# Sharing the last split row of a relu-and-sum kernel between ScalarE and VectorE, and cutting it in other places

## The chip, the cores and the metric

One core of a Trainium2 chip runs the whole program. Times are device microseconds (us) of that core. The span in the profile, from the first to the last recorded work of one execution, is shorter than the time by more than a microsecond. Engines are named as the profile names them: ACT is ScalarE, DVE is VectorE, SP is SyncE, which issues all transfers here.

## The reference

```
x: float32 [32, 512, 1024]            # 64 MiB
out = sum(max(x, 0), axis=-1)         # float32 [32, 512]
```

The 16,384 rows of 1,024 columns are laid over 128 partitions, so each partition has 128 rows. The last 16 of them, row 0 to row 15 below, are the last block, which the change is about.

## The kernel before

Seven loads of 16 rows (8 MiB) keep the transfer queue full. ScalarE clamps, VectorE sums, or either engine does both for one row with an accumulator output. The last block arrives in smaller and smaller loads, so that little work is left when the last bytes land: 8 rows, 4 rows, rows 12 and 13 with the first 360 columns of row 14, then row 15, then the rest of row 14 in pieces of 260 and 404 columns. Row 14 is the split row. VectorE sums its parts one after another; the closing instruction reads the last piece and, in the two columns behind it, the partial sums of the other parts (never negative, so the clamp leaves them as they are).

```
TAIL = [8, 4]
PIECES = [360, 260, 404]
...
    def dve_row(ap, accum_out, loaded):      # clamp and sum in one instruction
        i = nc.vector.tensor_scalar(out=ap, in0=ap, scalar1=0.0, scalar2=None,
                                    op0=MAX, op1=ADD, accum_out=accum_out)
        if loaded is not None:
            i.wait_op(loaded, 16, "sem-ge")
        i.then_inc(sems.dve, 1)
...
    first = PIECES[0]
    loaded = load(... rows 12, 13 and the first 360 columns of row 14 ...)
    act_row(buf[:, c, :], m, loaded)                              # row 12
    dve_row(buf[:, c + 1, :], res[:, m + 1 : m + 2], loaded)      # row 13
    last_loaded = load(buf[:, c + 3, :], rows(m + 3, 1)[:, 0, :]) # row 15
    arrived = []
    for part, w in zip(parts, PIECES[1:]):                        # 260, 404
        arrived.append(load(part[:, :w], rows(m + 2, 1)[:, 0, col : col + w]))
        col += w
    sums_done = n_act, n_dve
    act_row(buf[:, c + 3, :], m + 3, last_loaded)                 # row 15
    store(0, ROWS, *freed[0])
    store(ROWS, NT - ROWS - 2, *sums_done)
    last, w = parts[-1], PIECES[-1]
    dve_row(buf[:, c + 2, :first], last[:, w : w + 1], None)      # 360 columns
    for i in range(1, extra):
        dve_row(parts[i - 1][:, :], last[:, w + i : w + i + 1], arrived[i - 1])
    nc.vector.wait_ge(sems.dve, n_dve)        # own partial sums are written
    nc.vector.tensor_scalar(...last...).wait_op(arrived[-1], 16, "sem-ge")
    store(NT - 2, 2, n_act, n_dve)            # the last two results
```

## Time and profile before

| | before |
|---|---|
| time, median of 3 runs (range) | 161.35 us (161.24 to 161.53) |
| profiled execution: time, span | 160.99, 159.6 us |
| load queue's share of the transfer engines' time | 98.1% |
| VectorE, ScalarE busy | 74%, 65% |
| rows 12 and 13 land; row 13 starts | 155.34; 155.36 us |
| end of VectorE, end of ScalarE | 158.17, 157.81 us |

A load **lands** when its semaphore tells the waiting engine that the bytes are there. I call **the tail** the time from the start of row 13 on VectorE to the end of VectorE's last accumulator read: 158.17 - 155.36 = 2.81 us. The lines themselves, read from the end backwards, are in the prediction.

### The profile page before, as it was taken

The numbers are of one execution on the slowest core, as the hardware profiler recorded it, in microseconds if no ns is written. First come the engines' busy times: TensorE is split into PE (matmuls) and PEld (weight loads), VectorE is DVE, ScalarE is ACT, GpSimd is POOL, SyncE is SP. The second block draws the span as 40 slices with busy tenths as digits, with TensorE's granted clock in tenths as the row PEclk, the third lists the DMA queues.
The fourth block names the chain that finished last, engine by engine and source line by source line (L and its number), as shares of the span: only waits on it lengthen the run. The fifth ranks groups of instructions, "written<-read, shape, count | busy, mean of one in ns | idle before, by whom it ended". The sixth has DMA issues, their size and how long they took to land.

```text
span 159.6 us, 129 instructions
## 1 busy us (share of the span) xinstructions
DVE 117.5 (74%) x41; ACT 104.2 (65%) x50; POOL 0.2 (0%) x4
## 2 busy tenths in 40 slices
DVE  0000000009999499994999999999999999999986
ACT  3000059990799708996099941999339992499985
POOL 0000000000000000000000000000000000000000
DMA  7996996996996998979969969969969969798994
GB/s 263 525 525 263 525 526 263 525 525 263 526 493 296 525 411 378 525 328 460 526 279 509 525 263 526 525 263 525 525 263 525 509 279 525 337 452 386 412 405 127
DMA packets 2304, 67.18 MB, mean 421 GB/s; under 512 B 640, under 2 KB 896, under 8 KB 1024
## 3 DMA queue, kind: packets, MB, share of 16 engines
q1 hardware_dynamic: 2304, 67.18, 98.1%
HBM read 67.11 MB, written 0.07 MB: 421 GB/s over the span
## 4 chain that ended last, share of the span: by engine, by line
DMA 43%; DVE 34%; ACT 17%; another core or an unknown queue 3%; SPq 0%; issue 0%; DVEq 0%
DMA io<-in_x_dram 43%; DVE res L123 32%; ACT io L115 17%; DVE io L140 1%; SPq L97 0%; DVE piece L219 0%; DVE piece L140 0%; DVEq L218 0%
## 5 line engine op out<-in xcount | busy, mean ns | idle before, releaser
L123 DVE TENSOR_REDUCE res<-io 128x8 f32<-128x8192 f32 (+2 forms) x9 | 101.1, 11286 | 39.9 <-ACT io L115 39.9
L115 ACT ACTIVATE io<-io 128x8192 f32<-128x8192 f32 (+2 forms) x9 | 81.7, 9111 | 46.9 <-DMA io<-in_x_dram 46.9
L130 ACT ACTIVATE io<-io 128x1024 f32<-128x1024 f32 x20 | 20.9, 1045 | 5.9 <-DMA io<-in_x_dram 5.7
L140 DVE TENSOR_SCALAR_CACHE_REDUCE io<-io 128x1024 f32<-128x1024 f32 (+1 forms) x14 | 15.5, 1165 | 0.7 <-DMA io<-in_x_dram 0.6
L130 ACT ACTIVATION_READ_ACCUMULATOR io<-io 128x1 f32 x20 | 3.8, 188 | 0.0
L115 ACT ACT_TABLE_LOAD x1 | 1.3, 1283 | 0.8 <-PEq L260 0.8
L140 DVE DVE_READ_ACCUMULATOR io<-io 128x1 f32 x14 | 1.2, 82 | 0.0
L219 DVE TENSOR_SCALAR_CACHE_REDUCE piece<-piece 128x406 f32<-128x406 f32 x1 | 0.6, 576 | 0.1
L140 DVE TENSOR_SCALAR_CACHE_REDUCE piece<-piece 128x260 f32<-128x260 f32 x1 | 0.4, 424 | 0.0
L260 POOL MEMSET const-bfloat16-1.0<- 128x1 bf16 x1 | 0.1, 102 | 0.0
L260 POOL MEMSET const-uint8-127<- 128x1 uint8 x1 | 0.1, 102 | 0.0
L260 POOL MEMSET const-float32-0.0<- 128x1 f32 x1 | 0.1, 99 | 0.2 <-issue 0.2
L260 POOL MEMSET const-float32-1.0<- 128x1 f32 x1 | 0.1, 99 | 0.0
L140 DVE DVE_READ_ACCUMULATOR piece<-piece 128x1 f32 x1 | 0.1, 83 | 0.0
L219 DVE DVE_READ_ACCUMULATOR piece<-piece 128x1 f32 x1 | 0.1, 82 | 0.0
## 6 DMA issues: line engine op xcount, KB each, us to landing
io<-in_x_dram SPq DMA_DIRECT2D x1, 4096.0 KB, 21.6
io<-in_x_dram SPq DMA_DIRECT2D x1, 2048.0 KB, 26.1
io<-in_x_dram SPq DMA_DIRECT2D x1, 1204.0 KB, 28.6
io<-in_x_dram SPq DMA_DIRECT2D x1, 512.0 KB, 29.4
piece<-in_x_dram SPq DMA_DIRECT2D x1, 202.0 KB, 29.3
piece<-in_x_dram SPq DMA_DIRECT2D x1, 130.0 KB, 29.3
io<-in_x_dram SPq DMA_DIRECT2D x7, 26.9
out_dram<-res SPq DMA_DIRECT2D x1, 55.0 KB, 1.6
```

Source lines behind the costliest of these rows:

```text
L115: i = nc.scalar.activation(out=ap, in_=ap, func=RELU)
L123: nc.vector.tensor_reduce(out=res[:, m : m + n], in_=ap, axis=mybir.AxisListType.X, op=ADD).wait_op(sems.act, n_act, "sem-ge").then_inc(se ...
L130: i = nc.scalar.activation(out=ap, in_=ap, func=RELU, accum_out=res[:, m : m + 1])
L140: i = nc.vector.tensor_scalar(out=ap, in0=ap, scalar1=0.0, scalar2=None, op0=MAX, op1=ADD, accum_out=accum_out,)
L219: nc.vector.tensor_scalar(out=last[:, :], in0=last[:, :], scalar1=0.0, scalar2=None, op0=MAX, op1=ADD, accum_out=res[:, NT - 2 : NT - 1],) ...
L260: nc = _bacc.Bacc("TRN2", target_bir_lowering=False, num_devices=1)
```

## The change

The intent: ScalarE has a hole between row 12 and row 15. Let it take 180 columns of row 14 there, so that VectorE has less to do, and let the closing instruction be shorter (228 columns instead of 406). The load with rows 12 and 13 now brings 390 columns of row 14 (180 for ScalarE, 210 for VectorE), the last 190 columns come with row 15 in one load (they lie side by side in memory), and the middle comes last, as 220 and 224 columns.

```
-PIECES = [360, 260, 404]
+ACT_PIECE, DVE_PIECE, END_PIECE = 180, 210, 190
+PIECES = [220, 224]
...
+    loaded = load(flat[:, at : at + b], src[:, :b])            # rows 12, 13, 390 columns
+    act_row(buf[:, c, :], res[:, m : m + 1], loaded)
+    sums_act = n_act
+    act_row(flat[:, at + split : at + a], others[0], None)     # 180 columns, ScalarE
+    piece_act = n_act
+    dve_row(buf[:, c + 1, :], res[:, m + 1 : m + 2], loaded)
+    sums_dve = n_dve
+    dve_row(flat[:, at + a : at + b], others[1], None)         # 210 columns
+    loaded = load(flat[:, at + end : at + 4 * D], src[:, end:])# 190 columns and row 15
+    act_row(buf[:, c + 3, :], res[:, m + 3 : m + 4], loaded)
+    nc.vector.wait_ge(sems.act, piece_act)                     # ScalarE's partial sum
+    dve_row(flat[:, at + end : at + 3 * D], others[2], loaded) # 190 columns
...
-    dve_row(buf[:, c + 2, :first], last[:, w : w + 1], None)
-    for i in range(1, extra):
-        dve_row(parts[i - 1][:, :], last[:, w + i : w + i + 1], arrived[i - 1])
+    for i in range(len(PIECES) - 1):
+        dve_row(parts[i][:, :], others[3 + i], arrived[i])     # 220 columns
     nc.vector.wait_ge(sems.dve, n_dve)
... (closing instruction: 224 columns and four partial sums)
```

## The prediction

> **What bounds the kernel now.** I read first the page's busy shares and DMA table. VectorE is busy for 74% of the span, ScalarE for 65%, and the load queue for nearly all of it:
>
> ```profile
> q1 hardware_dynamic: 2304, 67.18, 98.1%
> ```
>
> The columns are packets, megabytes and the share of the 16 transfer engines' time. 67.11 MB must be read whatever is done at the end. The change moves not one byte of it. So only the tail, between the landing of the last bytes and the end of the last store, can shrink. I read that next, in the timeline from 155 us on (start, duration, engine, line, operation, output<-input, shapes):
>
> ```profile
> 155.36 1.06 ACT L130 ACTIVATE io<-io 128x1024 f32<-128x1024 f32 x1 [0.45 <-DMA io<-in_x_dram]
> 155.36 1.22 DVE L140 TENSOR_SCALAR_CACHE_REDUCE io<-io 128x1024 f32<-128x1024 f32 x1 [0.57 <-DMA io<-in_x_dram]
> ...
> 156.50 0.52 DVE L140 TENSOR_SCALAR_CACHE_REDUCE io<-io 128x360 f32<-128x360 f32 x1
> ...
> 156.65 1.06 ACT L130 ACTIVATE io<-io 128x1024 f32<-128x1024 f32 x1
> ...
> 157.02 0.42 DVE L140 TENSOR_SCALAR_CACHE_REDUCE piece<-piece 128x260 f32<-128x260 f32 x1
> 157.37 0.08 DVE L140 DVE_READ_ACCUMULATOR piece<-piece 128x1 f32 x1
> 157.58 0.58 DVE L219 TENSOR_SCALAR_CACHE_REDUCE piece<-piece 128x406 f32<-128x406 f32 x1
> 157.62 0.19 ACT L130 ACTIVATION_READ_ACCUMULATOR io<-io 128x1 f32 x1
> 158.09 0.08 DVE L219 DVE_READ_ACCUMULATOR piece<-piece 128x1 f32 x1
> ```
>
> The reader is to see that after the landing at 155.34 VectorE goes straight through row 13 and the three parts of row 14 (360, 260, then 404 columns with the two partial sums), and ends at 158.17. ScalarE has row 12, a hole of 0.15 us, row 15, and ends at 157.81, 0.36 us before VectorE. The last store starts after VectorE's end and lands 1.4 us later, at 159.6. Only the last VectorE end matters, as long as ScalarE stays before it.
>
> Third, when each piece landed. The issue of each piece, from two short windows of the timeline, and the list of issues (KB, us from issue to landing):
>
> ```profile
> 127.73 0.45 SPq L97 DMA_DIRECT2D piece<-in_x_dram  x1
> ```
> ```profile
> 128.22 0.50 SPq L97 DMA_DIRECT2D piece<-in_x_dram  x1
> ```
> ```profile
> piece<-in_x_dram SPq DMA_DIRECT2D x1, 202.0 KB, 29.3
> piece<-in_x_dram SPq DMA_DIRECT2D x1, 130.0 KB, 29.3
> ```
>
> So 260 columns land at 127.73 + 29.3 = 157.03, and the last 404 at 128.22 + 29.3 = 157.52. The same sum gives 155.34 for the load with rows 12 and 13 (issued 126.77, the chain's 28.57 us) and 156.65 for row 15 (issued 127.25, 29.4 us), and both are where the waiting instructions start. Last, the end of the chain that ended last:
>
> ```profile
> 157.47 0.03 issue
> 157.49 0.02 DVEq L218
> 157.51 0.07 issue
> 157.58 0.58 DVE piece L219 x2
> ```
>
> VectorE's own queue was ready for the last instruction at 157.51, the data at 157.52 within the rounding. **Two limits meet there:** the kernel before is balanced between transfer and VectorE, and taking from one alone is not enough.
>
> **What the Trainium skill says.** "ScalarE: Activation LUTs", section What ACT_TABLE_LOAD costs, gives 186 ns + 0.833 ns per column for an ACTIVATE without pointer operands, and an overlap of about 93 ns back to back. The trace agrees: 1042 ns for 1024 columns against 1039 ns; with the accumulator read of 187 ns starting 0.95 us in, rows repeat every 1.04 us. "VectorE: DVE Perf Modes", section The TRN2 errata, says that each instruction on SBUF pays a fixed extra latency, so many small pieces pay it many times. The trace has it: 424, 523, 576 and 1214 ns for 260, 360, 406 and 1024 columns is about 155 ns + 1.035 ns per column. Section The DRAIN says that a semaphore between two instructions of VectorE costs nothing extra; here I go by the trace, which differs: from the end of the 260 columns' accumulator read (157.45) to the start of the last instruction is 0.13 us, though part of that may be the landing at 157.52. "DMA: Bandwidth & Descriptors", Anatomy of one DMA, says a transfer's semaphore fires only after its last byte is confirmed; the trace shows load traffic falling to 10 GB/s by 157.0 to 157.2 us, with the landing at 157.52.
>
> **The change part by part.** I need VectorE's start-to-start step, not its duration. 1024 columns step by 1.14 us, and the accumulator read, which marks where the next may start, comes 0.45 us after the 360 columns and 0.35 us after the 260. That is 0.07 us + 1.045 ns per column.
>
> *Landings.* From 155.34 to 157.52, the remaining 512 + 130 + 202 KB landed, 864,256 bytes in 2.18 us, 396 GB/s. With this rate:
> - the first load now carries 390 columns instead of 360 of row 14, 15,360 bytes more: 155.34 + 0.04 = 155.38;
> - the second, 190 + 1024 columns, is 621,568 bytes, 1.57 us: 156.95 (row 15 landed at 156.65 before, so 0.30 us later);
> - 220 columns, 112,640 bytes, 0.28 us: 157.23;
> - 224 columns, 0.29 us: 157.52, as before, for the bytes are the same.
>
> *ScalarE.* Row 12 starts at 155.40; the 180 columns start 1.04 us later, at 156.44, and take 0.186 + 0.150 = 0.34 us; their accumulator read starts 0.09 us before that ends and takes 0.19, so the partial sum is there at 156.88. It was idle then, so this is **free**: it ends before 156.95. Row 15 then runs from 156.97 and by the same shape as before (1.16 us from start to the end of its read) ends at 158.13.
>
> *VectorE.* Row 13 at 155.40, the 210 columns at 156.54, done at 156.54 + 0.07 + 0.22 = 156.83. Now comes the new wait for ScalarE's 180 columns, passed at about 156.90; with the 0.02 us wait instruction and 0.07 us to the next start that the old wait shows, the 190 columns start at about 156.99, close to the 156.97 at which the data would allow it. They step by 0.27: 157.26. The 220 columns are there since 157.23, start at 157.26 and step by 0.30, and their accumulator read ends at 157.26 + 0.30 + 0.08 = 157.64. The old 0.13 us for the wait on the own partial sums gives 157.77. The last instruction has 224 + 4 = 228 columns, 0.07 + 0.24 = 0.31 us, and its read 0.08: **158.16, against 158.17 before.**
>
> *Sum.* ScalarE takes 180 x 1.045 ns = 0.19 us off VectorE. One more piece gives 0.07 us back. The rest goes to waits: before, row 14's first two parts ran in the time until 157.5 and no transfer held them by more than 0.07 us; now the 190 columns start about 0.15 us after VectorE could take them, since their load arrives with row 15's bytes. The last instruction starts 0.19 us later than before and is 0.19 us shorter. I therefore take 0.02 us off the 161.35 measured before and round: **161.32 us.**
>
> **The rivals.** *One: the last landing was the only limit*, and VectorE's chain gets ready by 157.52. Then the last instruction, 178 columns shorter, saves the whole 0.19 us, and ScalarE at 158.13 allows only about 0.04 of it: 161.30, or at best about 161.2 if row 15's load lands somewhat earlier than I reckon. For it speaks that landing and queue agree within 0.01 us before, so I can't tell which of the two cost the 0.07 us issue time. Against it: with 190 and 220 columns still to do after 156.95, VectorE needs 0.27 + 0.30 us and the closing wait, which is past 157.52 in any case. *Two: ScalarE becomes the bound.* Row 15 starts 0.3 us later than before; if its load of 4,856 bytes per partition lands 0.1 us later than by the mean rate, both ScalarE (158.23) and VectorE's 190 columns follow: 161.4 to 161.45. For it speaks that landing times follow the slowest of 16 transfer engines, not the mean. *Three: the wait of VectorE for ScalarE is dearer than reckoned*, for it stands in front of the 190 columns and all that follows goes later with it, one for one: 0.1 us more makes 161.45. *Four: pieces of 880 and 896 bytes per partition move worse than those of 1,040 and 1,616.* The 130 KB piece took 0.38 us, 350 GB/s, against 0.49 us for 202 KB, 422 GB/s. If both pieces go at 350, the last lands 0.06 us later, at 157.58, which is still before VectorE is ready; it would cost nothing.
>
> **Range and chances.** The routes span 161.2 to 161.45. The three runs before lie 0.29 us apart (161.24 to 161.53), more than the effect, so the measured median may be off by some 0.15 us either way. Together: 161.0 to 161.62 us. Two per cent is 3.2 us; the whole tail after the first of these landings (155.34 to 159.6) is 4.3 us, and nothing in the change reaches outside it. So within 2%: 0.99, and the remainder is left evenly to surprises such as a slower load order.
>
> **What would show it right or wrong.** In the changed profile: loads landing near 155.38, 156.95, 157.23 and 157.52 (order of bytes, at one rate); an ACTIVATE of 128x180 of about 0.34 us right behind row 12, with no wait; the 190 columns starting at 156.97 to 157.0; the closing instruction of 228 columns lasting about 0.39 us and starting near 157.77 rather than 157.58; VectorE's end within 0.1 us of 158.17; ScalarE's within 0.05 us of VectorE's, where it was 0.36 us ahead. The prediction is wrong if the last instruction starts by 157.6 (then the gain is real), if row 15 ends after VectorE by more than 0.1 us (then ScalarE is the bound), or if times before 155.3 move, which nothing in the change explains.

## The result, and the profile after

| | before | after |
|---|---|---|
| time, median (range) | 161.34 us (161.16 to 161.53), 6 runs | 161.39 us (161.26 to 161.50), 6 runs |
| ratio, 95% interval | | 1.0002 (0.9989 to 1.0015): same |
| span of the profiled execution | 159.6 us | 159.9 us |
| tail | 2.81 us (2.79 when run again) | 2.79 us (2.80 when run again) |

A ratio here is the mean time of one kernel's fast runs over that of the other's fast runs of the same rounds, so not quite the ratio of the medians quoted. The two tails can't be told apart: the traces of one kernel differ by up to 0.02 us.

The page after, in the line that answers to the first one of the prediction:

```profile
q1 hardware_dynamic: 2304, 67.18, 97.8%
```

Packets and bytes are the same; the queue is still what fills the span. The span is 0.3 us longer, and this is where a reader must be careful: the whole execution is shifted. Row 13 starts at 155.66 instead of 155.36 because the very first load, whose issue and 8 MiB the change doesn't touch, landed 0.30 us later (ScalarE's first large instruction starts at 22.03 instead of 21.73). So I subtract 0.30 before comparing. The timeline of the changed kernel from there on:

```profile
155.66 1.22 DVE L140 TENSOR_SCALAR_CACHE_REDUCE io<-io 128x1024 f32<-128x1024 f32 x1 [0.57 <-DMA io<-in_x_dram]
...
156.72 0.34 ACT L132 ACTIVATE io<-io 128x180 f32<-128x180 f32 x1
...
156.96 0.19 ACT L132 ACTIVATION_READ_ACCUMULATOR io<-io 128x1 f32 x1
157.10 0.08 DVE L140 DVE_READ_ACCUMULATOR io<-io 128x1 f32 x1
157.17 1.06 ACT L132 ACTIVATE io<-io 128x1024 f32<-128x1024 f32 x1
157.27 0.35 DVE L140 TENSOR_SCALAR_CACHE_REDUCE io<-io 128x190 f32<-128x190 f32 x1
157.55 0.08 DVE L140 DVE_READ_ACCUMULATOR io<-io 128x1 f32 x1
157.55 0.38 DVE L140 TENSOR_SCALAR_CACHE_REDUCE piece<-piece 128x220 f32<-128x220 f32 x1
157.85 0.08 DVE L140 DVE_READ_ACCUMULATOR piece<-piece 128x1 f32 x1
158.06 0.39 DVE L227 TENSOR_SCALAR_CACHE_REDUCE piece<-piece 128x228 f32<-128x228 f32 x1
158.13 0.19 ACT L132 ACTIVATION_READ_ACCUMULATOR io<-io 128x1 f32 x1
158.37 0.08 DVE L227 DVE_READ_ACCUMULATOR piece<-piece 128x1 f32 x1
```

See three things. ScalarE's 180 columns do run in its idle time (156.72), and their partial sum is written at 156.96 + 0.19 = 157.15. The 190 columns start only at 157.27, although VectorE could have taken them at 157.10. And the closing instruction is 0.19 us shorter than before (0.39 against 0.58) but starts 2.40 us after row 13, where it started 2.22 us after it before. What it gained in length it lost in its start.

The chain of waits of the changed kernel, in order of time (start, duration, what), names the two waits on VectorE's own queue (line 211 for ScalarE's partial sum, line 226 for its own):

```profile
155.66 1.52 DVE io L140 x4
157.18 0.00 issue
157.18 0.02 DVEq L211
157.20 0.07 issue
157.27 0.36 DVE io L140 x2
...
157.97 0.02 DVEq L226
157.99 0.07 issue
158.06 0.40 DVE piece L227 x2
```

This view leads to VectorE's own 210 columns, whose accumulator read ends at 157.18. ScalarE's partial sum, written at 157.15, is only 0.03 us earlier; that the wait for it is what holds the 190 columns is shown by experiments 2 and 3. No landing stands between. The last two loads (issue list; the issues started at 128.04 and 128.54) are

```profile
piece<-in_x_dram SPq DMA_DIRECT2D x1, 112.0 KB, 29.2
piece<-in_x_dram SPq DMA_DIRECT2D x1, 110.0 KB, 29.4
```

The list rounds to 0.1 us. By the trace's own landing times, 220 columns landed at 157.42 and the last 224 at 157.71, which is 0.35 us before the closing instruction starts. Before the change that margin was 0.07 us (157.51 to 157.58). The last step of the row is now VectorE's own chain.

### The profile page after: what moved, and what is told of

Same layout as the page of the kernel before. It is cut to its first block, busy times and chain, and to the rows that moved or that the text cites. A ratio compares the mean times of both kernels' runs of the same rounds, so it can differ in the third digit from the quotient of the medians.

```text
span 159.9 us, 134 instructions
## 1 busy us (share of the span) xinstructions
DVE 117.4 (73%) x43; ACT 104.5 (65%) x52; POOL 0.2 (0%) x4
## 4 chain that ended last, share of the span: by engine, by line
DMA 43%; DVE 34%; ACT 17%; another core or an unknown queue 3%; SPq 0%; issue 0%; DVEq 0%
DMA io<-in_x_dram 43%; DVE res L125 32%; ACT io L117 17%; DVE io L140 1%; SPq L99 0%; DVE piece L227 0%; DVE piece L140 0%; DVEq L226 0%; DVEq L211 0%
## 5 line engine op out<-in xcount | busy, mean ns | idle before, releaser
L132 ACT ACTIVATE io<-io 128x1024 f32<-128x1024 f32 (+1 forms) x21 | 21.2, 1010 | 5.8 <-DMA io<-in_x_dram 5.7
L140 DVE TENSOR_SCALAR_CACHE_REDUCE io<-io 128x1024 f32<-128x1024 f32 (+2 forms) x15 | 15.7, 1105 | 0.8 <-DMA io<-in_x_dram 0.6
## 6 DMA issues: line engine op xcount, KB each, us to landing
io<-in_x_dram SPq DMA_DIRECT2D x1, 1219.0 KB, 28.6
```

The source lines that it names most:

```text
L132: i = nc.scalar.activation(out=ap, in_=ap, func=RELU, accum_out=accum_out)
```

## The experiments

Twelve runs followed, two of them controls, in three groups of four, each group on another chip (experiments 1 to 4, 5 to 8 and 9 to 12). Each kernel was timed in five rounds beside the kernel before. All gave correct results. Since the first landing wanders by 0.3 us, the tail from the trace tells more than the time, and I quote both.

### 1. ScalarE's part alone

```
+ACT_PIECE = 180                     # PIECES stay 360, 260, 404; row 15 stays by itself
+    act_row(buf[:, c + 2, :ACT_PIECE], None, None, last[:, w + 2 : w + 3])
-    dve_row(buf[:, c + 2, :first], last[:, w : w + 1], None)
+    dve_row(buf[:, c + 2, ACT_PIECE:first], last[:, w : w + 1], None)
+    nc.vector.wait_ge(sems.act, piece_act)
```

> The kernel before, with only one part of the change: ScalarE takes 180 of the 360 columns that came with rows 12 and 13; loads, pieces of 260 and 404 and row 15 stay. I call the tail the time from the start of row 13 on VectorE to the end of VectorE's last accumulator read: 2.81 us before, 2.79 us after the change. Theory (transfers and the closing wait set the tail, VectorE's columns ahead of a landing are free): the 260 columns start at their landing, 1.67 us after row 13, as before (1.66), and the tail is 2.80 to 2.85 us. Rival (columns taken off VectorE count one for one, 180 x 1.04 ns): the tail is 2.62 us. Time as before, within 0.1 us, by the theory; 0.19 us less by the rival.

Measured: tail 158.34 - 155.53 = 2.81 us. The timeline:

```profile
157.20 0.42 DVE L141 TENSOR_SCALAR_CACHE_REDUCE piece<-piece 128x260 f32<-128x260 f32 x1 [0.18 <-DMA piece<-in_x_dram]
```

The 260 columns start at their landing, 1.67 us after row 13, and VectorE now stands idle 0.18 us before them: about the 0.19 us of the 180 columns that it no longer sums. Relief ahead of a landing turned into waiting for the landing, as the theory had it. But the time, 161.48 us against 161.21, ratio 1.0015 (1.0003 to 1.0028), is longer though the tail is the same. This I had not expected; it is taken up in experiments 5 to 11.

### 2. The wait for ScalarE moved behind

```
-    nc.vector.wait_ge(sems.act, piece_act)        # ahead of the 190 columns
     dve_row(flat[:, at + end : at + 3 * D], others[2], loaded)
...
+    nc.vector.wait_ge(sems.act, piece_act)        # ahead of the closing instruction
     nc.vector.wait_ge(sems.dve, n_dve)
```

> The changed kernel with VectorE's wait for ScalarE's partial sum moved from ahead of the 190 columns to ahead of the closing instruction, where it has long been met. Theory (this wait costs 0.09 us, because it is passed 0.02 us after the landing of row 15's load and the next start comes 0.07 us later): the 190 columns start 1.52 us after row 13 instead of 1.61, the 220 columns 1.80 instead of 1.89, the closing wait is passed accordingly, less up to 0.04 us for a second wait instruction; tail 2.70 to 2.75 us against 2.79. Rival (the landing of the load with row 15 is what holds the 190 columns, the wait is hidden behind it): they start at 1.58 or later, tail 2.77 to 2.83 us.

Measured: the 190 columns start 1.52 us after row 13 (155.54), the 220 columns 1.80 us, tail 2.75 us.

```profile
157.06 0.35 DVE L140 TENSOR_SCALAR_CACHE_REDUCE io<-io 128x190 f32<-128x190 f32 x1
```

So the wait for ScalarE cost the 190 columns 0.09 us; the landing would have let them go. Of the 0.09 us only 0.04 reach the end, since the queue now holds two waits in front of the closing instruction (the trace shows one queue instruction of 0.05 us instead of 0.02), and the closing instruction starts 0.55 us after the 220 columns instead of 0.51. Time 161.31 against 161.21 us, ratio 1.0013 (1.0000 to 1.0025).

### 3. Twice the columns on ScalarE

```
-ACT_PIECE, DVE_PIECE, END_PIECE = 180, 210, 190
+ACT_PIECE, DVE_PIECE, END_PIECE = 360, 30, 190
```

> The changed kernel with ScalarE's part doubled to 360 columns and VectorE's first part cut to 30, loads unchanged. It takes another 180 columns off VectorE and doubles the cost under suspicion. Theory (ScalarE's partial sum gates the 190 columns one for one): the partial sum comes 180 x 0.833 ns = 0.15 us later, so do the 190 columns (1.76 us after row 13 instead of 1.61) and all that follows on VectorE; row 15 starts where its load lands or up to 0.05 us later; tail 2.94 us against 2.79. Rival (VectorE's column count sets its end): 0.19 us less, tail 2.60 us. Second rival (the gate is hidden by landings): tail unchanged, 2.79 us.

Measured: tail 158.53 - 155.59 = 2.94 us, and the 190 columns start 1.76 us after row 13:

```profile
157.35 0.35 DVE L140 TENSOR_SCALAR_CACHE_REDUCE io<-io 128x190 f32<-128x190 f32 x1 [0.43 <-ACT io L132]
```

VectorE stands idle for 0.43 us, waiting for ScalarE. Taking another 180 columns off VectorE made the tail 0.15 us longer. Time 161.58 against 161.21 us, ratio 1.0023 (1.0009 to 1.0036). ScalarE's partial sum was written at 157.22, 1.63 us after row 13 instead of 1.48. This shows that it gates what follows one for one.

### 4. One closing piece of 444 columns

```
-PIECES = [220, 224]
+PIECES = [444]
```

> The changed kernel with its two middle pieces joined to one of 444 columns, so that the closing instruction has 447 columns instead of 228 and the row has one part less. Theory (after the change the closing instruction waits for VectorE's own chain, not for the last landing, and one part less takes its fixed 0.07 us and one closing wait out of the chain): the closing instruction starts within 0.05 us of the last landing, about 2.10 us after row 13 instead of 2.40, lasts 0.62 us instead of 0.39, tail 2.70 to 2.74 us against 2.79. Rival (the last landing sets the start of the closing instruction, so its length counts in full): it starts at 2.40 as now and the tail is 3.01 us, 0.22 us more.

Measured: tail 158.18 - 155.47 = 2.71 us, 0.08 less than after the change, although the closing instruction is 0.23 us longer. The end of the chain of waits:

```profile
157.52 0.04 issue
157.56 0.63 DVE piece L227 x2
```

The closing instruction starts 2.09 us after row 13 instead of 2.40, and this view puts the landing in front of it (127.82 + 29.7 = 157.52). VectorE's own queue was ready only 0.02 us earlier (its wait is passed at 157.50), so the two limits meet here again. After the change, then, the closing instruction was not waiting for data, and the shorter piece had bought nothing. Time 161.26 against 161.21 us, ratio 1.0002 (0.9989 to 1.0014): again 0.15 us or so longer than the shorter tail promises.

### 5 and 6. Controls: the kernel before and the changed kernel, each run once more

> A control: the kernel before, unchanged, run as if it were a new one. In the six traces so far the landing of the very first load (the start of ScalarE's first instruction) wanders between 21.73 and 22.03 us, with an unchanged stretch from there to row 13 (133.6 us). Theory (that wandering belongs to the execution, not to the kernel): ratio to the kernel before 1.000 within 0.0013, the first load lands at 21.7 to 22.05, and the tail (start of row 13 to VectorE's end) is 2.81 us again. Rival (something in the changed kernels delays their start): this one has its first landing at 21.73 within 0.05, below all the changed ones.

> The changed kernel again, on the same chip as the control. Theory: tail 2.79 us within 0.02, from the issue of the eight-row load to VectorE's end 32.24 us as in its first trace (32.25 in the kernel before); ratio 1.000 within 0.0015; first landing anywhere between 21.7 and 22.05. Rival (its start is late because of its own making): first landing at 22.0 again and a ratio of 1.001 or above.

Measured, the kernel before: 161.16 us, ratio 0.9999 (0.9987 to 1.0012), tail 2.79, first landing at 21.98, which is about as late as in the first trace of the changed kernel. Measured, the changed kernel: 161.43 us against 161.20, ratio 1.0016 (1.0003 to 1.0028), tail 2.80, from the issue of the eight-row load to VectorE's end 32.23 us, first landing at 21.79. So the late first landing belongs to the execution, not to the kernel. My expectation for the second ratio was missed, though: the changed kernel was 0.23 us longer with the same tail and no late landing.

The run lists say where. For each run there is a time and a span (to 0.1 us). Their difference, as mean over the runs, is 1.37 us for the nine runs of the kernel before in this group and 1.59 us for the five of the changed kernel, while the mean spans are 159.84 and 159.86 us. **The extra 0.22 us lies outside the profiled span**, where no view of the profile shows it. The same holds for experiments 1 to 4: their difference is 1.52 to 1.58 us, against 1.35 us for the kernel before in their group, so some 0.2 us of each one's time lies outside the span too.

### 7. The changed kernel without ScalarE's part

```
-ACT_PIECE, DVE_PIECE, END_PIECE = 180, 210, 190
+ACT_PIECE, DVE_PIECE, END_PIECE = 0, 390, 190
-    act_row(flat[:, at + split : at + a], others[0], None)
-    nc.vector.wait_ge(sems.act, piece_act)
```

> The changed kernel without its ScalarE part: VectorE takes all 390 columns that come with rows 12 and 13, there is no wait for ScalarE, and the closing instruction has one partial sum less (227 columns); loads unchanged. Theory (ScalarE's help is worth next to nothing, since the 190 columns can't start before their load lands 1.50 us after row 13 starts, and the wait for ScalarE costs 0.09 us on top): the 390 columns start 1.15 us after row 13 and step by 0.48 us, so the 190 columns start at 1.63 us instead of 1.61; tail 2.80 to 2.83 us against 2.79. Rival (180 columns off VectorE are worth 180 x 1.04 ns less one wait): the tail is 2.90 us or more.

Measured: tail 158.40 - 155.60 = 2.80 us, the 190 columns 1.62 us after row 13:

```profile
156.75 0.55 DVE L140 TENSOR_SCALAR_CACHE_REDUCE io<-io 128x390 f32<-128x390 f32 x1
...
157.22 0.34 DVE L140 TENSOR_SCALAR_CACHE_REDUCE io<-io 128x190 f32<-128x190 f32 x1
```

This undoes the half of the change that the title names first. VectorE takes all 390 columns and needs 0.47 us for them (start to start), instead of 0.29 us for 210, a 0.09 us wait for ScalarE and a pause. In the tail ScalarE's help, with its wait where the change put it, is worth 0.01 us at most, which is within the scatter of the traces. The time is 161.23 against 161.20 us, ratio 1.0001 (0.9987 to 1.0014), and the time less the span is 1.38 us: without ScalarE's extra instruction the 0.2 us outside the span are gone.

### 8. A rebalanced order that missed

Rows 12 and 13 by themselves, then 484 columns, row 15, 168 and 372 columns:

```
+ACT_PIECE, DVE_PIECE = 180, 304
+PIECES = [168, 372]
+    loaded = load(flat[:, at : at + split], src[:, :split])         # rows 12 and 13 only
+    loaded = load(flat[:, at + split : at + b], src[:, split:b])    # one load more
```

> A version meant to be better than both kernels, drawn from the readings: rows 12 and 13 land by themselves, earlier, which ends VectorE's and ScalarE's idle 0.45 to 0.57 us before them; then 484 columns of the split row (180 for ScalarE, 304 for VectorE), then row 15, then 168 columns, then the closing 372; the wait for ScalarE stands ahead of the 168 columns, where it has long been met. I measure from the issue of the eight-row load to VectorE's end: 32.25 us before, 32.24 after the change, 32.17 with one piece of 444. Theory: the closing instruction starts at the last landing (31.5 to 31.6), lasts 0.55, so VectorE ends at 32.08 to 32.16, ScalarE at about 32.05. Rival (one more load makes the last landing later): the last landing at 31.65 or later, VectorE's end at 32.25 or later. The time can hardly show it: 0.1 us is 0.06%, less than the interval of five rounds.

Measured: 32.29 us from the issue of the eight-row load to VectorE's end, against 32.23 to 32.26 in both kernels; time 161.46 against 161.20 us, ratio 1.0016 (1.0003 to 1.0028), of which some 0.19 us is again outside the span (1.55 us). My estimate missed and the rival came true. In the end of its chain of waits

```profile
128.92 28.91 DMA piece<-in_x_dram
157.83 0.02 issue
157.86 0.55 DVE piece L224 x2
```

the last piece lands at 157.83, 31.72 us after the eight-row load's issue (at 126.12), where it is 31.59 us in the kernel before and 31.50 us after the change. Row 13 did start earlier (155.12), but that didn't matter. That the extra load as such is what delays the last landing is likely, not shown: the order of the loads changed too.

### 9 to 11. What costs outside the span

An extra instruction on ScalarE that has nothing to do with row 14, eight of them, and an extra wait on VectorE, each added to the kernel before. With the extra instructions, ScalarE's first large instruction waits for ScalarE's own semaphore in place of the load's (not printed here); the kernel with eight has this too, so it isn't what costs 0.2 us.

```
+        for i in range(1 if j == 0 else 0):             # in the other kernel: 8
+            d = nc.scalar.activation(out=spare[...8 columns...], in_=buf[:, 0, :8],
+                                     func=RELU, accum_out=spare[...])
```
```
+    nc.vector.wait_ge(sems.act, sums_done[0])           # ahead of the 260 columns
     for i in range(1, extra):
```

> What is open: every kernel with ScalarE's extra piece has a time 1.52 to 1.59 us longer than its span on the mean of its runs, every one without it 1.35 to 1.39 us (the kernel before, its control, and the changed kernel without its ScalarE part). So the part costs about 0.2 us outside the profiled span. This run is the kernel before with one small ScalarE instruction (8 columns with an accumulator output, result unused) ahead of the first one, at 21.7 us, where 0.2 to 0.5 us delay is covered by later idle time; tail and VectorE untouched. Theory A (one instruction more in ScalarE's program costs it, wherever it stands): time less span 1.52 to 1.60 us; tail 2.81. Theory B (the extra piece at the end or the extra wait on VectorE does it): 1.34 to 1.40 us.

> As the run with one extra ScalarE instruction, with eight of them. They delay ScalarE's first large instruction by 8 x 0.2 us, which idle time later covers. Theory A1 (a step, once the program is longer than some size): time less span 1.52 to 1.60, as with one. Theory A2 (a cost for each instruction): 2.5 us or more. Theory B: 1.34 to 1.40.

> The kernel before with one more wait for ScalarE on VectorE, ahead of the 260 columns, long met when it is reached (row 12 is done 0.5 us earlier). Theory A (ScalarE's program length is what costs outside the span): time less span 1.34 to 1.40. Theory B (the wait on VectorE does it): 1.52 to 1.60. For the tail: the wait stands ahead of a landing and is met, so the 260 columns start at their landing, 1.66 us after row 13, and the tail stays 2.81 us; if a met wait costs its 0.09 us all the same, 1.70 and about 2.85.

| kernel | ScalarE instructions | tail, us | time less span, mean of runs, us | median time, us |
|---|---|---|---|---|
| before (nine runs of this group) | 50 | 2.81 (first trace) | 1.36 | 161.16 |
| one extra ScalarE instruction | 52 | 2.80 | 1.56 | 161.47 |
| eight extra | 66 | 2.78 | 1.37 | 161.46 |
| extra wait on VectorE | 50 | 2.81 | 1.36 | 161.13 |
| change without ScalarE's part (group 2) | 50 | 2.80 | 1.38 | 161.23 |
| the change (first rounds; group 2) | 52 | 2.79; 2.80 | 1.57; 1.59 | 161.39; 161.43 |

(The profile counts an instruction with an accumulator output as two, and 66 is 50 + 16.) One small ScalarE instruction at 22 us, far from the tail, brings the 0.2 us back: theory A of that run holds, and neither the place of the instruction nor the wait on VectorE is the cause. But eight of them cost nothing outside the span, so it is neither a step nor a cost for each, and the run misses both A1 and A2. It matches theory B's number, but B is excluded by the run with one. The eight instructions have a longer time for a visible reason: their mean span is 160.14 us against 159.84, and in the trace each of the last loads lands 0.3 to 0.4 us later after its issue (the one with rows 12 and 13 after 28.9 us instead of 28.6). I had written that idle time would cover their delay; it did not. The extra wait was passed at 156.71 us, 0.04 us after row 12's sum and long before VectorE was free for the 260 columns (157.12). It shows no cost in the tail: these start 1.67 us after row 13, at their landing, which would hide a cost of up to 0.07 us.

### 12. A version drawn from these readings

```
-ACT_PIECE, DVE_PIECE, END_PIECE = 180, 210, 190
-PIECES = [220, 224]
+ACT_PIECE, DVE_PIECE, END_PIECE = 0, 390, 190
+PIECES = [444]
```

> A version meant to beat both kernels: the changed kernel without its ScalarE part (VectorE takes 390 columns) and with one closing piece of 444 columns. Theory: the 390 columns end as the 190 columns' load lands, these start 1.62 us after row 13, the closing instruction (446 columns) at the last landing or at 2.10, whichever is later, tail 2.70 to 2.75 us against 2.81 and 2.79; time less span 1.34 to 1.40, as there is no ScalarE part; so about 161.1 us, 0.1 below the kernel before and 0.3 below the changed one. Rival (without ScalarE's help the 390 columns hold the chain up): closing start at 2.20 or later, tail 2.82 or more.

Measured: tail 158.32 - 155.59 = 2.73 us, closing instruction 2.11 us after row 13, time less span 1.38 us, time 161.08 us (160.99 to 161.17) against 161.16, ratio 0.9991 (0.9979 to 1.0004). The trace is as expected and the mean span is 159.70 us against 159.84. The time is not shown to be better than the kernel before, for the interval holds 1. Against the changed kernel there was no run in the same group; by way of the kernel before it would be some 0.25% shorter by group 2 (ratio 1.0016) and 0.1% by the first rounds (1.0002), each on another chip, so this isn't shown either.

## Why the prediction was right or wrong

The verdict (same, 161.32 us predicted, 161.39 measured) was right, and the mechanism in the tail is shown. Two sums of the prediction don't come out: 158.16 against 158.17 is 0.01 us, and 161.35 less the 0.02 that it took is 161.33. Its sign of being wrong, "times before 155.3 move", did appear (0.30 us), but the control shows that this belongs to the execution. Point by point:

- **Two limits meet before the change.** Right that taking from VectorE alone is not enough: experiment 1 relieved it ahead of a landing and the tail stayed at 2.81 us, with 0.18 us of new idle time. Which of the two set the closing start, the prediction left open; the traces settle it. In experiment 8, where the landing came last, the closing instruction starts 0.02 us behind it, as the chain shown there has it. In the kernel before it starts 0.07 us behind both the landing and the queue's wait (157.51 to 157.58), as it does behind the wait alone after the change (157.99 to 158.06). So the queue's wait set it, and the landing would have allowed a start some 0.05 us earlier (an estimate from these two steps). The landing that did hold VectorE is that of the 260 columns (157.00, start 157.02).
- **Landings.** The order and the same bytes were right, the rate slightly low. Measured, less the shift of 0.30 us: 155.34, 156.85, 157.12 and 157.41, against 155.38, 156.95, 157.23 and 157.52. The 848,896 bytes behind rows 12 and 13 took 2.07 us, about 410 GB/s instead of 396. So the last landing was not "as before" but 0.09 us sooner; nothing waited for it, so this gained nothing.
- **ScalarE's 180 columns are free.** In ScalarE's own time, yes: the partial sum came at 156.85 by the shifted clock, 156.88 predicted. "ScalarE: Activation LUTs" of the Trainium skill, section What ACT_TABLE_LOAD costs, agrees for a short instruction too: 186 ns + 0.833 ns x 180 = 336 ns against 0.34 us measured. For VectorE, no: the load of the 190 columns came 0.10 us sooner than reckoned, so these could have started that much sooner, and the wait for ScalarE took it away (experiment 2). The wait was not dearer than reckoned (reached at 156.88 by the shifted clock, 156.90 predicted), so rival three did not come true; that a later partial sum would move all that follows one for one, as it says, experiment 3 shows.
- **VectorE's starts.** 190 columns 156.97 (156.99 predicted), 220 columns 157.25 (157.26), closing 157.76 (157.77), end 158.15 (158.16). That these agree to 0.02 us although the landing was off is because the wait for ScalarE, not the landing, set the first of them.
- **Rival one, the last landing as the only limit,** is out: 0.35 us lie between that landing and the closing instruction, and experiment 4 gains by a longer piece.
- **Rival two, ScalarE as the bound,** is out: it ended 0.13 us before VectorE (158.32 against 158.45; 0.03 predicted), since row 15's load landed sooner than reckoned.
- **Rival four, that the smaller pieces move worse,** is out: from one landing to the next, 112,640 bytes took 0.27 us and 114,688 took 0.29 us, about 416 and 393 GB/s, not 350.
- **The step that failed** is "nothing in the change reaches outside it", said of the tail. The ScalarE instruction costs about 0.2 us outside the span. With it the sum would have been 161.35 - 0.02 + 0.2 = 161.5 us, and the rounds of group 2, 161.43 against 161.20 us, bear that out. The first rounds show only 0.05 us between the medians. The scatter of the runs may have hidden the rest, but the spans of the six runs of the kernel before are not on record there, so this is not shown. That the predicted number lies within 0.07 us of the first result is thus in part luck.

**Where the expected gain went**, then: 0.19 us of summing were taken off VectorE. Nearly all of it is back in the 190 columns' start, first as their load's landing and then as the wait for ScalarE; undoing ScalarE's part changes the tail by 0.01 us. The 0.19 us by which the closing instruction got shorter went into the two pieces and the two queue waits that now stand in front of it.

**What stays open** is why ScalarE's program with 52 instructions has a time 0.2 us further from its span than with 50 or 66. It held in all eight sets of runs with 52 (1.52 to 1.59 us, means of five or six runs) against 1.35 to 1.39 with 50 or 66. The count of all engines' profiled instructions is not the reason: 131 both with one extra instruction (1.56 us) and in the change without ScalarE's part (1.38 us). "Runtime: NRT & Kernel Launch" of the Trainium skill, section Instruction fetch mechanics, describes a block-wise fetch of each engine's instructions whose cost it calls mostly hidden; no run here shows whether this has to do with it. The final value of ScalarE's semaphore changed with the count as well and was not tried apart.

## What to carry to other kernels

Work taken off an engine ahead of a landing was worth nothing here (tail 2.81 us with and without it), since the landing came no earlier; look for the wait that ends last at each step, and at the end weigh a shorter last piece against the extra step and queue wait that it puts in front of itself. Waiting for another engine's partial sum later, where it had long been there, gave 0.04 us back. When the trace and the time disagree, compare time less span between kernels before looking for the cause inside the trace.

## What the Trainium skill lacked or had wrong

- No page that I read has a cost outside the span that depends on one engine's instruction count: 1.52 to 1.59 us of time beyond the span with 52 ScalarE instructions, 1.35 to 1.39 with 50 and 66. "Runtime: NRT & Kernel Launch", section The ~15µs preamble/postamble breakdown, calls the gap between the profile's total and the reported execution time kernel-invariant; that gap is taken between other quantities (about 6.2 us there), so this is a lack and not a contradiction.
- "VectorE: DVE Perf Modes", section The DRAIN, has eight copies take the same time with a semaphore after each as with one after the last, and says that the semaphore costs nothing extra there. A wait passed long before VectorE is free fits that: an extra one left the 260 columns at 1.67 us and the tail at 2.81 us. The page has no cost for a wait that holds VectorE: the runs show 0.09 us from the queue's instruction to the next start (157.18 to 157.27), and 0.12 us with a second wait in front (157.77 to 157.89).
- "DMA: Bandwidth & Descriptors" gives no number for how the last landing moves when the end of a queue is cut into other loads: from the eight-row load's issue to the last landing, 31.58 to 31.61 us in five traces with the loads of the kernel before (31.95 with the eight extra instructions, where all the last loads came later), 31.50 to 31.53 in five with those of the change, 31.47 and 31.51 with one piece of 444 columns, 31.72 with one load more.
